# Tiles of a two-layer decoder moved to multiples of 512 bytes in the on-chip memory

## The chip, the cores and the metric

The kernel runs on one core of one Trainium2 chip. Its time is the device time of one execution in microseconds (us). A core has TensorE (PE: matrix products; PEld is its load of the stationary operand), VectorE (DVE), ScalarE (ACT), GpSimd (POOL) and SyncE (SP, which here issues most DMAs). They work side by side, each in the order of its own queue, and share an on-chip memory of 128 partitions. A tile has 128 rows, one to a partition, and takes the same bytes in each; its place is its first byte within the partition.

## The reference

x has 512 tokens of 2,048 channels in float32. Two layers follow each other; each norms x, projects it with one wide matrix, works on the columns by branches, gates the branches with SiLU, projects them back and adds the result to x.

```python
for layer in range(DEPTH):
    h = rmsnorm(x, norm_gains[layer])
    if layer % 2 == 0:
        x = x + even_layer(h, *even_params)
    else:
        x = x + odd_layer(h, *odd_params)
return rmsnorm(x, final_norm_gain)
```

The even layer has a gated linear recurrence (RG-LRU, width 1,024, with a short convolution and two gates) and attention over a window of 128 keys with sinks (16 query heads). The odd layer has multi-head latent attention (MLA: low-rank queries and keys/values, rotary part, 8 heads) and differential attention (two softmaxes of which the second is subtracted, 8 heads). Its projections are all products of 512 tokens with 2,048 (or 768, or 512) channels.

## The kernel before

Activations stand transposed: 128 channels on the partitions, 512 tokens along the row. One output tile of a projection is a `Job`: 16 steps over the 2,048 input channels, at each step the product of a 128x128 block of weights (stationary, loaded into the array) with a 128x512 activation tile (streamed), added up in one bank of the output memory. For the accuracy of float32 from float32r products, each operand is kept as a rounded high part and the rest (low part), and a step is three products (`mm3`): high·high, high weight·low activation, low weight·high activation.

Weights come as pieces of 128x1024 (`Piece`). A piece is loaded into a tile `wr`; ScalarE copies it rounded into `wh`, VectorE subtracts into `wl`. These three have three buffers each in the pool `wts`. Pieces that are used twice at the end ("kept") and those of the MLA values are split into ordinary work tiles instead (`sh`, `sl`). All activations, their high and low parts (`sh`/`sl`, `yh`/`yl`, `ch`/`cl`, `xh`/`xl`, `kh`/`kl`), scores and probabilities are work tiles of 2,048 bytes: 76 buffers of the pool `work`. The gates of the recurrence have their own pool `gatew`: `xp` (the convolution's input with three columns of zeros ahead), `gw` (gate weights) and `gh`, `gl` (their parts). The opening differs from the rest: the first two output tiles (`o`) are computed with both operands in work tiles, while x and the first weights (`fr`) arrive.

The order of instructions on PE, ACT and DVE is written by the program itself: a small planner with fixed costs runs the tasks of the attention branches between the steps of the jobs. Where a tile lies is no part of the plan.

The pools lie one behind the other in the order in which they are made: `const`, `wts`, `gatew`, `work`, `tiny`. A tile takes its size, rounded up to 32 bytes. So the sizes in `const` and `gatew` decide where the tiles behind them begin. Before the change `const` holds, among others, `cc` (constants: identity, ones, masks, cosines), `onesr`, `g0`, `idle` (zeros for the nine warm-up products at the start) and, made later, `junk` (an output nobody reads).

In a row of the profile `mm<-sh,wh` means: output tile mm, streamed operand sh, stationary operand wh. `mm`, `o`, `sc` and `pt` are the output banks. All instructions pass through one line of a helper (L61), so groups are told apart by tiles.

Of the kernel before, what the change touches and what calls it, by code (L numbers as in the profile page):

```python
# [9 lines left out]
F32 = mybir.dt.float32  # L10
# [5 lines left out]
P = 128  # L16
S = 512
# [6 lines left out]
NSLOT = 76  # L24
WARM = 9
DEBUG = False


C_G0, C_G1, C_GF = 0, 16, 32
# [162 lines left out]
def trunk_kernel(ctx: ExitStack, tc, xT, w0, w0o, wg, w1, wuq, wuk, wuv, w1o, small, cst, outT):  # L192
# [11 lines left out]
    gp = ctx.enter_context(tc.tile_pool(name="gatew", bufs=2))  # L204
# [9 lines left out]
    def nm(s):  # L214
        count[0] += 1
        return f"{s}_{count[0]}"
# [7 lines left out]
    def const(n, name, dt=F32):  # L224
        return cp.tile([P, n], dt, name=nm(name))[:, :]
# [172 lines left out]
    def big_job(wt, m, X, done, pre=None, norm=None, kept=(False, False), tag="mm"):  # L398
        return Job(big_parts(wt, m, kept), X, done, pre, norm, tag)
# [73 lines left out]
    pool.memset(nhalf, -0.5)  # L473
    onesr = const(P, "onesr", F32R)
    g0 = const(KT, "g0")

    def col(c):
        return sm[:, c : c + 1]


    idle = const(P, "idle")
    dve.memset(idle, 0.0)
    warm = bank("sc")
    for _ in range(WARM):
# [56 lines left out]
    def parameters():  # L541
# [37 lines left out]
        dve.tensor_tensor(hp, hp, sr, ALU.mult)  # L579
        dve.scalar_tensor_tensor(sp4, hp, 2.0, relu, ALU.mult, ALU.add)  # L580
        dve.tensor_scalar(sp4, sp4, 4.0, None, ALU.mult)

    junk = const(P, "junk")

    def evac(acc, norm, name):
        z = wk(name)
        dve.tensor_tensor(z, acc, norm.r, ALU.mult)
        return z
# [62 lines left out]
    def lru(t, xp, gw):  # L651
        xc = wk("xc")
        cw = [col(C_CW + 8 * j + t) for j in range(4)]
        yield after(xp, sp4)
        dve.tensor_scalar(xc, xp[:, 0:S], cw[0], col(C_CB + t), ALU.mult, ALU.add)
        for j in range(1, 4):
            dve.scalar_tensor_tensor(xc, xp[:, j : j + S], cw[j], xc, ALU.mult, ALU.add)
        gh = gp.tile([P, 2 * P], F32R, name=nm("gh"), tag="gh", bufs=1)[:, :]
        gl = gp.tile([P, 2 * P], F32R, name=nm("gl"), tag="gl", bufs=1)[:, :]
        high(gh, gw)  # L660
        yield after(gh, xc)
        low(gl, gw, gh)
        xh, xl = wk("xh", F32R), wk("xl", F32R)
        high(xh, xc)
        yield after(xh)
        low(xl, xc, xh)
        yield after(xl)
        gi, th = wk("gi"), wk("th")
        for j, (dst, b) in enumerate(((gi, C_GXB), (th, C_GAB))):
            a = []  # L670
            yield from take("sc", a)
            mm3(a[0], gh[:, j * P : (j + 1) * P], gl[:, j * P : (j + 1) * P], (xh, xl), True, True)
            yield after(a[0])
            act.activation(dst, a[0], AF.Sigmoid, bias=col(b + t))
            give("sc", a[0])
        act.activation(th, th, AF.Tanh, scale=sp4[:, t : t + 1])
        yield after(gi)
        dve.scalar_tensor_tensor(gi, gi, 2.0, xc, ALU.mult, ALU.mult)
        yield after(th)
        rec = wk("rec")  # L680
        dve.tensor_scalar(rec, th, 1.0, None, ALU.add)
        dve.reciprocal(rec, rec)
        sq = wk("sqt")
        act.activation(sq, th, AF.Sqrt)
        yield after(sq, rec)
        dve.tensor_tensor(sq, sq, rec, ALU.mult)
        dve.tensor_scalar(rec, rec, 2.0, -1.0, ALU.mult, ALU.add)
        dve.tensor_tensor(gi, gi, sq, ALU.mult)
        h = wk("h")
        dve.tensor_tensor_scan(h, rec, gi, 0.0, ALU.mult, ALU.add)  # L690
        hs[t] = h
# [111 lines left out]
    def gates0(t, za, zb):  # L803
        while t not in hs or t not in os_:
            yield plan.now + 0.5
        yield after(za, zb)
        act.activation(za, za, AF.Silu)
        act.activation(zb, zb, AF.Silu)
        yield after(za, hs[t])
        dve.tensor_tensor(za, hs[t], za, ALU.mult)  # L810
        yield after(zb, os_[t])
        dve.tensor_tensor(zb, os_[t], zb, ALU.mult)
        Y0[2 * t] = za
        Y0[2 * t + 1] = zb
        hs[t] = os_[t] = 0

    def layer0_jobs(t):
        def x_done(acc):
            xp = gp.tile([P, S + 4], F32, name=nm("xp"), tag="xp", bufs=1)[:, :]
            dve.memset(xp[:, 0:3], 0.0)  # L820
            dve.tensor_tensor(xp[:, 3 : 3 + S], acc, n0.r, ALU.mult)
            gw = gp.tile([P, 2 * P], F32, name=nm("gw"), tag="gw")[:, :]
            pool.dma_start(gw, wg[t])
            plan.spawn(lru(t, xp, gw))

        def q_done(acc):
            plan.spawn(swa(t, evac(acc, n0, "qz")))

        zs = []

        def g_done(acc):
            zs.append(evac(acc, n0, "gz"))
            if len(zs) == 2:
                plan.spawn(gates0(t, *zs))

        big_job(w0, 2 + 4 * t, X0, x_done, None, n0)
        big_job(w0, 4 + 4 * t, X0, q_done, None, n0)
        yield
        big_job(w0, 3 + 4 * t, X0, g_done, None, n0, tag="mm" if t else "pt")
        big_job(w0, 5 + 4 * t, X0, g_done, None, n0)  # L840
        yield
# [510 lines left out]
    for i, j in enumerate(jobs):  # L1352
# [3 lines left out]
        elif j is not skip:  # L1356
            j.run()
        if DEBUG:
            print("job", i, "%.1f" % plan.now)
# [128 lines left out]
```

## Time and profile before

| | |
|---|---|
| median of 3 runs | 1594.34 us (1594.31 to 1594.49) |
| the profiled execution | 1594.0 us |
| its span, first to last instruction | 1592.2 us |
| mean granted TensorE clock | 0.997 |
| PE busy | 1576.4 us (99%), 7,450 products |
| PEld busy | 1296.6 us (81%) |
| DVE busy | 867.1 us (54%) |
| ACT busy | 705.2 us (44%) |
| DMA | 156.11 MB, mean 98 GB/s |

A product's listed duration runs from its start to the end of its writing; the next one starts before that end. How fast PE gets through a row of products is therefore read from their starts, or from a window: its length over the number of products that start in it. In a window's row the columns are PE, PEld, DVE, ACT and POOL, each with its busy time and the number of instructions that ran in it, then the granted clock, the DMA engines' busy share and GB/s.

### The profile page before, as it was taken

What the parts mean: (1) busy time and instruction counts of PE and PEld (TensorE: products, weight loads), DVE (VectorE), ACT (ScalarE), POOL (GpSimd) and SP (SyncE); (2) the same over time, 40 slices, a digit from 0 to 9 for tenths busy, and PEclk for the clock granted to TensorE, in tenths of its full rate; (3) what the DMA queues carried; (4) which work ended last, traced back from release to release, by engine and by line L of the source; (5) the groups of instructions that cost most, each with busy time, mean ns of one, the idle gap of its engine ahead of it and who ended that gap; (6) DMA issues with size and microseconds to landing.
All of it is one profiled execution on the core that took longest, in us unless ns stands there. A gap on an engine that the chain in (4) does not pass through costs nothing.

```text
span 1592.2 us, 19224 instructions
## 1 busy us (share of the span) xinstructions
PE 1576.4 (99%) x7450; PEld 1296.6 (81%) x7450; DVE 867.1 (54%) x1603; ACT 705.2 (44%) x1219; POOL 48.2 (3%) x76
## 2 busy tenths in 40 slices
PE   9999999999999999999999999999999999999996
PEld 7888888888888888888888888888888888888886
DVE  7877676677853334455445555542344365843344
ACT  7466455556643323444444454432323356632222
POOL 0000000000001100000000000000000000010000
PEclk9999999999999999999999999999999999999998
DMA  8222232222334443222222222222322221342323
GB/s 282 87 78 91 80 96 83 83 80 80 102 117 147 136 152 105 89 82 83 87 80 79 80 82 89 81 80 93 95 91 86 77 75 55 113 139 93 97 89 106
DMA packets 48922, 156.11 MB, mean 98 GB/s; under 512 B 5552, under 2 KB 9792, under 8 KB 48704
## 3 DMA queue, kind: packets, MB, share of 16 engines
q1 hardware_dynamic: 44576, 141.25, 27.8%
q0 software_dynamic: 4256, 13.64, 2.6%
q8 instruction: 58, 0.95, 0.2%
q14 instruction: 32, 0.26, 0.1%
HBM read 146.49 MB, written 8.39 MB: 97 GB/s over the span
## 4 chain that ended last, share of the span: by engine, by line
PE 97%; issue 1%; DVE 1%; DMA 0%; SPq 0%; POOLq 0%; ACT 0%; POOL 0%; DVEq 0%
PE mm L61 85%; PE o L61 5%; PE sc L61 5%; PE pt L61 3%; DMA xin<-in_xT 0%; DVE st L61 0%; SPq L61 0%; DVE sl L61 0%; POOLq L1483 0%; ACT sh L61 0%; POOL rcf L61 0%; DVE mg L61 0%; DVE yl L61 0%; DVE dg L61 0%; DVEq L1483 0%
## 5 line engine op out<-in xcount | busy, mean ns | idle before, releaser
L61 DVE TENSOR_TENSOR wl<-wr,wh 128x1024 fp32r<-128x1024 f32 (+1 forms) x244 | 290.9, 1192 | 436.3 <-ACT wh L61 436.1
L61 PE MATMUL mm<-sh,wh 128*128 128x512 f32 x1312 | 528.2, 403 | 0.0
L61 PE MATMUL mm<-sl,wh 128*128 128x512 f32 x1312 | 518.4, 395 | 0.0
L61 PE MATMUL mm<-sh,wl 128*128 128x512 f32 x1312 | 518.4, 395 | 0.0
L61 ACT ACTIVATE wh<-wr 128x1024 fp32r<-128x1024 f32 (+1 forms) x244 | 252.2, 1034 | 425.1 <-PE mm L61 342.2
L61 PEld LDWEIGHTS mm<-sh,wl 128*128 128x128 f32 x1312 | 246.2, 188 | 59.3
L61 PEld LDWEIGHTS mm<-sh,wh 128*128 128x128 f32 x1312 | 246.8, 188 | 50.7
L61 PEld LDWEIGHTS mm<-sl,wh 128*128 128x128 f32 x1312 | 246.8, 188 | 50.2
L61 PE MATMUL mm<-yh,wh 128*128 128x512 f32 x448 | 177.7, 397 | 0.0
L61 PE MATMUL mm<-yh,wl 128*128 128x512 f32 x448 | 177.1, 395 | 0.0
L61 PE MATMUL mm<-yl,wh 128*128 128x512 f32 x448 | 177.1, 395 | 0.0
L61 DVE CUSTOM_DVE_ANT_0 p<-sc,cc 128x128 f32<-128x128 f32 (+3 forms) x96 | 47.0, 490 | 98.8 <-PE sc L61 98.6
L61 PEld LDWEIGHTS mm<-yh,wl 128*128 128x128 f32 x448 | 84.1, 188 | 20.4
L61 PEld LDWEIGHTS mm<-yh,wh 128*128 128x128 f32 x448 | 84.1, 188 | 20.1
L61 PEld LDWEIGHTS mm<-yl,wh 128*128 128x128 f32 x448 | 84.1, 188 | 20.0
L61 ACT ACTIVATE p<-p,negm 128x128 f32<-128x128 f32 (+3 forms) x96 | 53.8, 560 | 68.9 <-DVE negm L61 67.4
L61 ACT ACT_TABLE_LOAD x50 | 64.2, 1283 | 1.5 <-PEq L1479 0.7
L61 ACT ACTIVATE aT<-pt 128x128 f32<-128x128 f32 (+3 forms) x64 | 27.6, 435 | 62.0 <-PE pt L61 61.8
L61 ACT ACTIVATE sq<-xr 128x512 f32<-128x512 f32 (+1 forms) x33 | 19.3, 586 | 55.1 <-DVE xr L61 55.1
L61 PE MATMUL mm<-ch,wh 128*128 128x512 f32 x104 | 42.0, 404 | 0.0
L61 DVE TENSOR_TENSOR ss<-ss,sq 128x512 f32<-128x512 f32 (+1 forms) x54 | 36.0, 667 | 10.2 <-ACT sq L61 9.4
L61 PE MATMUL mm<-cl,wh 128*128 128x512 f32 x104 | 41.1, 395 | 0.0
(253 smaller groups left out, 1820.4 us busy)
## 6 DMA issues: line engine op xcount, KB each, us to landing
wr<-in_w SPq DMA_DIRECT2D x166, 512.0 KB, 3.5
wr<-in_w0o SPq DMA_DIRECT2D x32, 512.0 KB, 3.6
wr<-in_w1o SPq DMA_DIRECT2D x32, 512.0 KB, 3.5
wr<-in_wuq SPq DMA_DIRECT2D x12, 384.0 KB, 3.1
xin<-in_xT SPq DMA_DIRECT2D x16, 256.0 KB, 5.4
xr<-in_xT POOLq DMA_DIRECT2D x16, 256.0 KB, 3.7
x1d<-xr POOLq DMA_DIRECT2D x16, 256.0 KB, 3.5
xr<-x1d POOLq DMA_DIRECT2D x16, 256.0 KB, 3.0
```

Source lines behind the costliest of these rows:

```text
L61: return f(*args, **kw)
```

## The change

Three things are done to places; the instructions of every engine and their order stay as they were, but for the name of one tile. `idle` and `junk` become one tile, made where `idle` was. A tile of 96 columns (384 bytes) that nothing uses, `gap`, is put into `const`. `xp` gets 128 columns more than its 512 instead of 4.

```diff
+XPAD = 128
...
     g0 = const(KT, "g0")
+    const(96, "gap")
...
-    idle = const(P, "idle")
+    idle = junk = const(P, "junk")
     dve.memset(idle, 0.0)
...
-    junk = const(P, "junk")
-
...
-            xp = gp.tile([P, S + 4], F32, name=nm("xp"), tag="xp", bufs=1)[:, :]
+            xp = gp.tile([P, S + XPAD], F32, name=nm("xp"), tag="xp", bufs=1)[:, :]
```

Where the first buffers begin, worked out from the sizes of all tiles (bytes within a partition, and what is left over a multiple of 512):

| tiles | before | rest | after | rest |
|---|---|---|---|---|
| cc | 18112 | 192 | 18112 | 192 |
| onesr | 26336 | 224 | 26336 | 224 |
| wr, wh, wl (each buffer 4,096) | 28288 | 128 | 28160 | 0 |
| xp | 65152 | 128 | 65024 | 0 |
| gw, gh, gl (each 1,024) | 67232 | 160 | 67584 | 0 |
| work tiles (each 2,048) | 71328 | 160 | 71680 | 0 |

Sizes of wts, gw and work buffers are multiples of 512, so what holds for the first buffer holds for all, and for each 128-column block (512 bytes) within one.

## The prediction

> **What bounds the kernel now.** I read the page's busy shares and the chain that ended last first, to see which engine sets the end; then the groups of instructions by shape, to see what that engine does; then the timeline and windows of TensorE, to measure the step from one product's start to the next. The last is needed because products are pipelined: their listed durations overlap.
>
> ```profile
> PE 1576.4 (99%) x7450; PEld 1296.6 (81%) x7450; DVE 867.1 (54%) x1603; ACT 705.2 (44%) x1219; POOL 48.2 (3%) x76
> PEclk9999999999999999999999999999999999999998
> PE 97%; issue 1%; DVE 1%; DMA 0%; SPq 0%; POOLq 0%; ACT 0%; POOL 0%; DVEq 0%
> PE mm L61 85%; PE o L61 5%; PE sc L61 5%; PE pt L61 3%; DMA xin<-in_xT 0%; DVE st L61 0%; SPq L61 0%; DVE sl L61 0%; POOLq L1483 0%; ACT sh L61 0%; POOL rcf L61 0%; DVE mg L61 0%; DVE yl L61 0%; DVE dg L61 0%; DVEq L1483 0%
> L61 PE MATMUL mm<-sl,wh 128*128 128x512 f32 x1312 | 518.4, 395 | 0.0
> L61 PE MATMUL mm<-yl,wh 128*128 128x512 f32 x448 | 177.1, 395 | 0.0
> L61 PE MATMUL mm<-cl,wh 128*128 128x512 f32 x104 | 41.1, 395 | 0.0
> ```
>
> TensorE carries 97% of the chain, at a granted clock of nine tenths or more in all slices but the last, and 85% of the chain is one kind of work: 512-wide products into "mm" with a streamed operand from the work pool (sh, sl, yh, yl, ch, cl) and stationary weights from a weight piece (wh, wl). Each of the three groups shown has two sisters of the same count, so there are 3 x (1312 + 448 + 104) = 5,592, and 48 more into "pt": 5,640. A change acts through the step of these 5,640 products or hardly at all.
>
> That step has two values in this trace:
>
> ```profile
> 15.31 0.39 PE L61 MATMUL o<-sh,sl 128*128 128x512 f32 x1
> ...
> 28.91 0.39 PE L61 MATMUL o<-sh,sl 128*128 128x512 f32 x1
> ```
>
> ```profile
> 15.30:28.90 13.60, 13.60 (x61) 11.27 (x60) 12.77 (x20) 11.62 (x20) 0.00 (x0) 1.00 0.93 350
> 440.00:620.00 180.00, 180.00 (x773) 144.81 (x772) 75.32 (x89) 57.78 (x72) 15.03 (x28) 1.00 0.42 135
> 1259.18:1267.57 8.39, 8.39 (x38) 6.95 (x37) 3.21 (x6) 3.40 (x6) 0.00 (x0) 1.00 0.17 50
> ```
>
> A window counts the product already running at its start, so x61 is 60 starts. In the opening, where streamed and stationary operand both lie in the work pool (160 bytes past a multiple of 512), 13.60 us / 60 = 226.7 ns. In the output projection of layer 0, with the stationary operand in a weight piece (128 past), 180.00 / 772 = 233.2 ns. In the MLA value products, both operands in the work pool again, 8.39 / 37 = 226.8 ns. All are 512-wide, at clock 1.00. The fast opening is the busiest stretch of all (DVE 12.77 and ACT 11.62 of 13.60 us, DMA share 0.93), the slow one is quieter, so other engines and transfers are not what costs the 6.5 ns. Nor is the output bank: the value products fill one bank for twelve products, as the slow ones do for 48.
>
> The cleanest piece of evidence is a few products of the recurrence's gates (gh and gl lie at 160) that stand inside the stream of weight pieces:
>
> ```profile
> 67.07 0.40 PE L61 MATMUL mm<-sh,wl 128*128 128x512 f32 x1
> 67.31 0.39 PE L61 MATMUL sc<-xh,gh 128*128 128x512 f32 x1
> 67.53 0.39 PE L61 MATMUL sc<-xl,gh 128*128 128x512 f32 x1
> 67.76 0.40 PE L61 MATMUL sc<-xh,gl 128*128 128x512 f32 x1
> 67.99 0.40 PE L61 MATMUL mm<-sh,wh 128*128 128x512 f32 x1
> ```
>
> ```profile
> 67.54 0.19 PEld L61 LDWEIGHTS sc<-xh,gl 128*128 128x128 f32 x1
> 67.76 0.19 PEld L61 LDWEIGHTS mm<-sh,wh 128*128 128x128 f32 x1
> L61 PE MATMUL sc<-xh,gh x16: 388/390/398, 67.3 to 390.1; 128*128 128x512 f32 x16
> L61 PE MATMUL sc<-xh,gl x16: 390/396/397, 67.8 to 390.6; 128*128 128x512 f32 x16
> ```
>
> The load of the next stationary operand (PEld) starts with the running product: gl is loaded from 67.54 under xl·gh, which began at 67.53; the next wh from 67.76 under xh·gl. A product under which a tile at 160 is loaded takes 390 ns, like the fast stretches; the third, under which a wh at 128 is loaded, 396 ns. (The timeline's starts round to 10 ns; these medians show the 6 ns better.) So the slow step goes with the place of the operand being loaded, against that of the one being streamed.
>
> **The change part by part.** Instructions, order, waits and transfers stay; only places in the on-chip memory move.
>
> Weight pieces go from 128 to 0 past a multiple of 512, work tiles and gate weights from 160 to 0. Streamed and loaded operand of every big product then have the same place within 512 bytes, as in the fast stretches. If that sameness is what counts, each of the 5,640 steps goes from 233.2 to 226.7 ns: 6.5 x 5,640 = 36.7 us less. That is on the path, since PE is 97% of it. Not all will come, because the fast step does not always set in at once after another shape:
>
> ```profile
> 1329.70 0.39 PE L61 MATMUL mm<-sl,ch 128*128 128x512 f32 x1
> ...
> 1330.63 0.39 PE L61 MATMUL mm<-sh,cl 128*128 128x512 f32 x1
> ```
>
> Between these starts lie four steps, with both operands at 160, just after transposes: 0.93 / 4 = 232 ns. In the timeline of PE the 512-wide products stand in 428 runs; 1,568 products are among the first six of a run, 938 among the first three. With no gain but 1.2 ns on the first six, 4,072 x 6.5 + 1,568 x 1.2 = 28.4 us; the gates, where the fast step sets in at once, speak for the full 36.7. Middle: 32 us.
>
> The 256-wide products of the tail and of the scores go the other way, or stay:
>
> ```profile
> 1542.46 0.28 PE L61 MATMUL mm<-yh,sh 128*128 128x256 f32 x1
> ...
> 1547.98 0.28 PE L61 MATMUL mm<-yl,sh 128*128 128x256 f32 x1
> 1542.45:1547.99 5.54, 5.54 (x49) 5.54 (x48) 3.67 (x5) 2.63 (x4) 0.00 (x0) 1.00 0.01 3
> 1553.78 5.61 PE o L61 x48
> ```
>
> With both operands in the work pool (two of the 49 were already running, so 47 starts and 46 steps) it is 5.52 / 46 = 120.0 ns; with wh at 128 (48 in the chain's last row) 5.61 / 48 = 116.9. Only 96 products are of the second kind: 96 x 3.1 = +0.3 us.
>
> VectorE and ScalarE: their operands move as well. The split of a kept piece reads at 128 and writes at 160, a sum of squares has all at 160, and they take the same:
>
> ```profile
> L61 DVE TENSOR_TENSOR sl<-wr,sh 128x512 fp32r<-128x512 f32 x20 | 12.8, 686 | 3.1 <-ACT sh L61 3.1
> L61 DVE TENSOR_TENSOR ss<-ss,sq 128x512 f32<-128x512 f32 x50 | 34.4, 687 | 9.3 <-ACT sq L61 8.4
> L61 DVE TENSOR_TENSOR wl<-wr,wh 128x1024 fp32r<-128x1024 f32 x224 | 273.9, 1223 | 409.4 <-ACT wh L61 409.2
> ```
>
> I cost them at nothing. Their cover is TensorE itself: the split of the pieces waits 409 us in all for the copy ahead of it, which in turn waits for work of PE, so a PE faster by 2% leaves DVE at 867 / 1560 = 56%. The one tile that now serves for warm-up and scratch, the gap and the wider xp add no instruction: nothing.
>
> Sum, against the profiled execution's own 1594.0 us (span 1592.2 and 1.8 around it; the median of the runs is 1594.34): 1594.3 - 32 + 0.3 = 1562 us, or 1558 to 1566 between the two bounds.
>
> The bounds of what no row shows, a product whose streamed operand starts at a multiple of 64 or more: every streamed float32r operand here starts at 160. From 256 to 512 columns the fast step grows by 226.7 - 120.0 = 106.7 ns, so columns alone are 213.4 of the 226.7 ns and 13.3 ns stand on top in both. The lower bound is that these vanish, the upper that nothing changes or that the 3.1 ns of the 256-wide products are added. I take 226.7, the value that same-place operands have.
>
> [...]
>
> **The rivals.** First, more than the fast step. The 13.3 ns on top may come from the streamed tile's odd start itself: if the memory is read in pieces of 64 bytes (sixteen columns), 2,048 bytes from 160 touch one piece more than from 0, and sixteen columns cost 213.4 x 16 / 512 = 6.7 ns, half of the 13.3. If one such piece goes, about 6,700 products of 256 columns and more (5,640, and some 1,050 from the work and gate pools) save 6.7 ns beside the 32 us: 45 us more, 1517. If all 13.3 go, 89 us, 1473. For it: 13.3, and the 6.5 of the slow step, are nearly whole multiples of 6.7. Against: the constant is as well explained by the load, and no row has an aligned stream.
>
> [...]
>
> Second, no change. The load may be slow at even multiples of 64 bytes (128 now, 0 then) and fast at odd halves (160), whatever the stream does; then the 5,640 steps stay at 233.2 and it is 1594. For it: the trace varies only the loaded operand, never the streamed one. Against: a worse time for the rounder place would be odd, unless two streams meet.
>
> Third, slower. The 256-wide products lose 3.1 ns where places agree. If agreement costs that in every product, and the fast stretches are fast for the odd start of their load, the big steps go to 236.3: 5,640 x 3.1 = 17.5 us, 1612. It decides once the step is over 233.8 ns (3.2 us / 5,640 = 0.6 ns more). For it the tail's rows, against it the 226.8 of the value products, whose places agree.
>
> **How the numbers follow.** The fast step taking over, 1558 to 1566: 0.47. More than that, 1473 to 1550: 0.33 (most of it near 1517, 0.05 below 1487). Part of it, because the fast step seldom sets in after an interruption, 1568 to 1590: 0.05. No change: 0.08. Slower: 0.07. A measurement of this kernel can tell about 0.2%, 3.2 us. Faster 0.85, same 0.08, slower 0.07. The likeliest gives 1562. The range leaves out the two last cases and the lowest of the second: 1487 to 1590.
>
> **What would show it.** Right: windows at the output projections with 226.7 ns a step or less, the listed 395 ns of mm<-sl,wh at 390 or less, VectorE's 686 and 1223 ns as they were, PE still 97% of the chain. The 96 tail products at 120 say that agreement is the rule. [...] I am wrong if PE's step falls and the span does not, because waits of PE on DVE or ACT, which hardly show in the chain now, take its place.

## The result, and the profile after

| | before | after |
|---|---|---|
| median | 1594.41 us (1594.31 to 1595.1, 4 runs) | 1567.35 us (1565.43 to 1567.61, 4 runs) |
| the profiled execution | 1594.0 us | 1567.61 us |
| its span | 1592.2 us | 1565.8 us |

The ratio is 0.9827, 95% interval 0.981 to 0.9844: 27 us less. 1562 had been forecast, with 1558 to 1566 for the likeliest case; the time lies just past that and inside the range.

The page's first line and its chain say that the bound is the same engine:

```profile
PE 1549.5 (99%) x7450; PEld 1297.9 (83%) x7450; DVE 866.4 (55%) x1603; ACT 705.2 (45%) x1219; POOL 48.2 (3%) x76
...
PE 97%; issue 1%; DVE 1%; DMA 0%; SPq 0%; POOLq 0%; ACT 0%; POOL 0%; DVEq 0%
```

PE's busy time fell by 26.9 us, DVE's by 0.7 and ACT's not at all. The groups of products and of VectorE's splits (mean duration after the busy time):

```profile
L62 PE MATMUL mm<-sl,wh 128*128 128x512 f32 x1312 | 512.0, 390 | 0.0
L62 PE MATMUL mm<-yl,wh 128*128 128x512 f32 x448 | 174.5, 389 | 0.0
L62 PE MATMUL mm<-cl,wh 128*128 128x512 f32 x104 | 40.6, 391 | 0.0
L62 DVE TENSOR_TENSOR sl<-wr,sh 128x512 fp32r<-128x512 f32 x20 | 12.8, 686 | 3.1 <-ACT sh L62 3.1
L62 DVE TENSOR_TENSOR wl<-wr,wh 128x1024 fp32r<-128x1024 f32 x224 | 273.6, 1222 | 392.5 <-ACT wh L62 392.3
```

The three kinds of big product that took 395 ns take 389 to 391; the splits take what they took (686 and 1223 ns before). A window inside the output projection of layer 0 and the pieces of the chain that hold the long stretches give the step. The chain before, for comparison:

```profile
437.57 189.00 PE mm L61 x810
...
1059.28 103.58 PE mm L61 x444
```

The window and the chain after:

```profile
440.00:600.00 160.00, 160.00 (x707) 132.30 (x706) 67.08 (x79) 51.13 (x63) 14.49 (x27) 1.00 0.44 142
```

```profile
432.55 183.75 PE mm L62 x810
...
1043.03 100.69 PE mm L62 x444
...
1527.51 5.76 PE o L62 x48
```

160.00 / 706 = 226.6 ns a step, where it was 233.2. The same 810 products that took 189.00 us of the chain take 183.75. The last row is the tail's 48 products of 256 columns: 5.76 / 48 = 120.0 ns, where it was 116.9.

### The profile page after: what moved, and what is told of

Read it like the earlier page. It is cut to its first block, busy times and chain, and to the rows that moved or that the text cites. A ratio compares the mean times of both kernels' runs of the same rounds, so it can differ in the third digit from the quotient of the medians.

```text
span 1565.8 us, 19224 instructions
## 1 busy us (share of the span) xinstructions
PE 1549.5 (99%) x7450; PEld 1297.9 (83%) x7450; DVE 866.4 (55%) x1603; ACT 705.2 (45%) x1219; POOL 48.2 (3%) x76
## 3 DMA queue, kind: packets, MB, share of 16 engines
q1 hardware_dynamic: 44576, 141.25, 28.4%
## 4 chain that ended last, share of the span: by engine, by line
PE 97%; issue 1%; DVE 1%; DMA 0%; SPq 0%; POOLq 0%; ACT 0%; POOL 0%; DVEq 0%
PE mm L62 84%; PE o L62 5%; PE sc L62 5%; PE pt L62 4%; DMA xin<-in_xT 0%; DVE st L62 0%; SPq L62 0%; DVE sl L62 0%; POOLq L1483 0%; ACT sh L62 0%; POOL rcf L62 0%; DVE mg L62 0%; DVE yl L62 0%; DVE dg L62 0%; DVEq L1483 0%
## 5 line engine op out<-in xcount | busy, mean ns | idle before, releaser
L62 PE MATMUL mm<-sh,wh 128*128 128x512 f32 x1312 | 522.5, 398 | 0.0
L62 PE MATMUL mm<-sh,wl 128*128 128x512 f32 x1312 | 512.3, 390 | 0.0
L62 PE MATMUL mm<-sl,wh 128*128 128x512 f32 x1312 | 512.0, 390 | 0.0
```

The source lines that it names most:

```text
L62: return f(*args, **kw)
```

## The experiments

All of them keep the instructions and their order and differ from the change only in places. The comparison kernel in each is the one before the change. "Place" below is the rest over a multiple of 512 bytes. The chain has in each the piece of 810 products without another shape between them, so its length is the measure of the step: 810 x 226.7 = 183.6 us or 810 x 233.3 = 189.0.

**Which of the places counts.** Two runs take away one half of the change each (the wider `xp`, or `gap`), two put the places elsewhere.

gap_only: weight pieces at 0, gates and work tiles at 32.

```diff
-XPAD = 128
+XPAD = 4
```

> The change without the wider xp: weight pieces at 0 past a multiple of 512, work tiles and gates at 32. Theory P (the step depends on whether the loaded and the streamed operand have the same place): they differ by 32, so 233.2 ns a step at the projections, 1593 to 1596 us, and the 96 tail products with wh at 116.9 ns. Theory W (the loaded operand at a multiple of 512 is enough): 226.7 ns, 1565 to 1568 us.

xp_only: everything at 128.

```diff
-    const(96, "gap")
```

> The change without the gap of 96 columns: weight pieces, gates and work tiles all at 128 past a multiple of 512. Theory P: the places agree, 226.7 ns, 1565 to 1568 us, tail products 120.0 ns. Theory M (the multiple of 512 itself counts, or 128 is a bad place for weights): 233.2 ns, 1593 to 1596 us.

all160: everything at 160.

```diff
-    const(96, "gap")
+    const(136, "gap")
```

> Weight pieces, gates and work tiles all at 160 past a multiple of 512, an odd multiple of 32. Theory P: 226.7 ns, 1565 to 1568 us. Theory M (the multiple of 512, or of 64, counts): 1593 to 1596 us.

w32_x0: weight pieces at 32, gates and work tiles at 0.

```diff
-XPAD = 128
+XPAD = 120
...
-    const(96, "gap")
+    const(104, "gap")
```

> Weight pieces at 32 past a multiple of 512, work tiles and gates at 0. Theory P: they differ by 32, 233.2 ns, 1593 to 1596 us. Theory S (the streamed operand at a multiple of 512 is enough): 226.7 ns, 1565 to 1568 us.

| run | weights | work | median us | ratio to before (95%) |
|---|---|---|---|---|
| gap_only | 0 | 32 | 1593.96 | 0.9997 (0.9988 to 1.0007) |
| xp_only | 128 | 128 | 1566.8 | 0.9829 (0.9814 to 0.9844) |
| all160 | 160 | 160 | 1565.99 | 0.9823 (0.9808 to 0.9837) |
| w32_x0 | 32 | 0 | 1594.55 | 1.0 (0.9991 to 1.001) |

The chain's piece of 810 products and, where shown, the tail's 48, in that order of the runs:

```profile
437.68 188.99 PE mm L62 x810
...
1554.04 5.61 PE o L62 x48
```

```profile
430.63 183.78 PE mm L62 x810
...
1526.01 5.76 PE o L62 x48
```

```profile
431.04 183.78 PE mm L62 x810
```

```profile
438.41 189.00 PE mm L62 x810
...
1554.62 5.67 PE o L62 x48
```

Theory P holds four times out of four. Each half of the change alone either gives nothing (gap_only) or all of it (xp_only), according to whether the places agree. Weights at a multiple of 512 are not enough, work tiles at a multiple of 512 are not enough, and with everything at an odd multiple of 32 the whole gain is there. The price in the tail has the other sign: 5.76 us where places agree, less where they don't (5.61 in gap_only, 5.67 in w32_x0).

**Within what unit they must agree.** The weights at 64, 128 and 256, work tiles at 0 (the gap grows by 64, 128 and 256 bytes, xp shrinks by as much):

```diff
-XPAD = 128
+XPAD = 112    # w64_x0; 96 in w128_x0; 64 in w256_x0
...
-    const(96, "gap")
+    const(112, "gap")    # w64_x0; 128 in w128_x0; 160 in w256_x0
```

> Weight pieces at 64 past a multiple of 512, work tiles and gates at 0. If places need to agree within 64 bytes only (Q64): 226.7 ns a step, 1565 to 1568 us. If they need to agree within 128 to 512 bytes (Q512): 233 ns, 1592 to 1596 us.

> Weight pieces at 128 past a multiple of 512, work tiles and gates at 0. If places must agree within a unit of 128 bytes only: 226.7 ns a step, 1565 to 1568 us. If within 256 or 512: 233.3 ns, 1592 to 1596 us.

> Weight pieces at 256 past a multiple of 512, work tiles and gates at 0. If places must agree within a unit of 256 bytes: 226.7 ns a step, 1565 to 1568 us. If within 512: 233.3 ns, 1592 to 1596 us.

w64_x0 took 1595.8 us (ratio 1.0011, 1.0001 to 1.002), w128_x0 1591.63 us (0.9983, 0.9972 to 0.9994), w256_x0 1565.2 us (0.9815, 0.9787 to 0.9844). Their pieces of the chain:

```profile
438.17 188.99 PE mm L62 x810
```

```profile
437.20 188.22 PE mm L62 x810
```

```profile
429.92 183.79 PE mm L62 x810
```

So of the distances tried the unit is 256 bytes: a difference of 256 is as good as none, 128 is nearly as bad as 64. w256_x0 (two runs) is the fastest median of all, but its interval overlaps that of the change; the two can't be told apart, and no run beats the change beyond that.

**How exactly they must agree.** First try: the buffers of wh and wl 64 bytes longer, the parts 4 or 16 bytes in. It rested on a unit of 64 bytes, which w64_x0 refuted: buffers 64 bytes longer lie at 64, 128, ... to each other, so all but one of the six differ from the work tiles for that reason already. The two runs are inconclusive on what was asked.

```diff
+OFF = 1    # off4B; 4 in off16B
...
-            t = wp.tile([P, 1024], dt, name=nm(tag), tag=tag)[:, :]
+            t = (wp.tile([P, 1024], dt, name=nm(tag), tag=tag)[:, :] if tag == "wr" else
+                 wp.tile([P, 1040], dt, name=nm(tag), tag=tag)[:, OFF : OFF + 1024])
...
-    const(96, "gap")
...
```

The last cut, here and in the second try, is the tile `st` near the end, which uses the same buffers and is lengthened with them.

> High and low weight parts start 4 bytes past a multiple of 64 (each buffer is 64 bytes longer), work tiles at 0. If agreement to the element counts: 233 ns or more, 1592 us or more. If 16 or 32 bytes are the unit in which places agree: 226.7 ns, 1565 to 1568 us.

> High and low weight parts start 16 bytes past a multiple of 64, work tiles at 0. If 32 bytes are the unit: 226.7 ns, 1565 to 1568 us. If 16 bytes or less are the unit: another step than 226.7 ns; between 226.7 and 233.3 if the price grows with the distance, 1567 to 1594 us.

off4B took 1592.3 us (0.9987, 0.9976 to 0.9997), off16B 1591.07 us (0.9982, 0.9972 to 0.9992).

Second try: buffers longer by 512 bytes, so that all places stay equal but for the offset; two work slots fewer pay for the room.

```diff
-NSLOT = 76
+NSLOT = 74
...
+OFF = 1    # far_off4B; 4 in far_off16B
...
-            t = wp.tile([P, 1024], dt, name=nm(tag), tag=tag)[:, :]
+            t = (wp.tile([P, 1024], dt, name=nm(tag), tag=tag)[:, :] if tag == "wr" else
+                 wp.tile([P, 1152], dt, name=nm(tag), tag=tag)[:, OFF : OFF + 1024])
...
```

> Buffers of wh and wl 512 bytes longer (paid for with two work slots fewer, order of instructions unchanged), and the weight parts start 4 bytes past a multiple of 512; work tiles at 0. If one element of distance already counts: 232 to 233.3 ns a step, 1590 to 1596 us. If places are compared in units of 16 or 32 bytes: 226.7 ns, 1565 to 1569 us.

> As the run with 4 bytes, with the weight parts 16 bytes past a multiple of 512. If 16 bytes already count: 232 to 233.3 ns a step, 1590 to 1596 us. If places are compared in units of 32 bytes: 226.7 ns, 1565 to 1569 us.

far_off4B took 1590.31 us (0.9974, 0.9962 to 0.9986), far_off16B 1587.68 us (0.9954, 0.9932 to 0.9977). The chain, 4 bytes first; the piece of 638 holds the output projection of layer 1:

```profile
436.91 188.23 PE mm L63 x810
```

```profile
436.81 189.00 PE mm L63 x810
...
1412.98 134.76 PE mm L63 x638
```

The piece of 638 before the change, and after it:

```profile
1415.43 138.35 PE mm L61 x638
```

```profile
1392.68 134.83 PE mm L62 x638
```

One element of distance costs most of the gain: about 4 us of the 27 are left. With 16 bytes the trace gives two answers. The output projection of layer 0 (the piece of 810) is as slow as before the change, and that of layer 1 is as fast as after it, all through its piece: 134.76 us. That is 3.6 of the 6.8 us by which the run is faster than before, and so a little faster than either branch of the expectation allowed for. At this distance, then, the rest over 256 bytes alone does not decide the step; what does is open. The two work slots fewer had no control of their own.

**Is the price paid load by load.** wl_off32 moves only the low weight parts, by 32 bytes put ahead of them (xp shrinks by as much):

```diff
-XPAD = 128
+XPAD = 120
...
+            if tag == "wl" and not slots[tag]:
+                wp.tile([P, 8], F32, name=nm("pad"), tag="pad", bufs=1)
             t = wp.tile([P, 1024], dt, name=nm(tag), tag=tag)[:, :]
```

> As the change, but with the low parts wl alone at 32 past a multiple of 512 (32 unused bytes ahead of them); everything else at 0. One load in three then differs from the stream. If each load prices the product that runs over it (D): a mean step of (2 x 226.7 + 233.3) / 3 = 228.9 ns, 5,640 / 3 x 6.6 = 12 us over the change, 1577 to 1581 us. If one load that differs spoils the steps that follow (T): 232 to 233 ns, 1588 to 1595 us.

It took 1592.91 us (0.9992, 0.9982 to 1.0001). The chain, a window at the output projection of layer 0, the groups of products between 445 and 600 us, and four products of that stretch:

```profile
437.61 188.98 PE mm L62 x810
```

```profile
440.00:600.00 160.00, 160.00 (x687) 128.64 (x686) 67.69 (x81) 52.13 (x65) 13.99 (x26) 1.00 0.41 135
```

```profile
L62 PE MATMUL mm<-yl,wh 128*128 128x512 f32 x222 | 88.8, 400 | 0.0
L62 PE MATMUL mm<-yh,wh 128*128 128x512 f32 x222 | 87.7, 395 | 0.0
L62 PE MATMUL mm<-yh,wl 128*128 128x512 f32 x222 | 86.4, 389 | 0.0
```

```profile
502.77 0.40 PE L62 MATMUL mm<-yl,wh 128*128 128x512 f32 x1
503.01 0.39 PE L62 MATMUL mm<-yh,wl 128*128 128x512 f32 x1
503.24 0.40 PE L62 MATMUL mm<-yh,wh 128*128 128x512 f32 x1
503.47 0.40 PE L62 MATMUL mm<-yl,wh 128*128 128x512 f32 x1
```

The product under which wl is loaded (yl·wh) takes 400 ns, the one after it 389 and the third 395. The starts go the same way: the median step over this projection is 239 ns after the start of yl·wh, 228 after yh·wl and 233 after yh·wh. So the price is not the same at every step: it is doubled under the load that is out of place, nearly nothing at the next step and single at the third. The mean is 160.00 / 686 = 233.2, as if every load were out of place. Of the two expectations the number of T came out, and D's 228.9 did not; T's picture, one bad load that makes all following steps slow, did not come out either. Why the three steps add up to the full price is open.

## Why the prediction was right, and where it was off

**The bound** was read rightly: PE carries 97% of the chain before and after, and no wait took the place of what went. That the time lies inside 1487 to 1590 says little by itself, since the lower part of that range was there for a rival that did not come true; what bears the prediction out is the step. No run shows a step that would lead to the range's lower end of 1487 us or below it; the whole gain came with 226.6 to 226.9 ns.

**The step.** 226.7 ns was taken from the opening and the value products; 226.6 was measured. That the gain comes from agreement, and not from round places, is shown by xp_only and all160 against gap_only and w32_x0. The gates' products, which had no neighbour of another place after the change, went the same way, the third kind from a median of 396 to 389:

```profile
L62 PE MATMUL sc<-xh,gh x16: 388/389/396, 68.6 to 385.7; 128*128 128x512 f32 x16
L62 PE MATMUL sc<-xh,gl x16: 389/389/397, 69.2 to 386.2; 128*128 128x512 f32 x16
```

"Within 512 bytes" was too coarse (the unit is 256), and the gates' rows read as a price paid by the product under the load: wl_off32 shows the price largest there (239 ns), but paid by another product of the three as well, so that it can't be counted load by load.

**The term that was mis-sized** is the one for short runs of products. The prediction took 32 us, the middle between 28.4 (no full gain on the first six of a row) and 36.7. The upper bound rested on the gates, and these do not bear on the term: 15 of their 16 groups stand behind other 512-wide products, not behind another shape. The lower bound was the better reading: added up over the timeline's PE rows, the 5,640 products take 28.6 us less (mean step 235.1 ns before, waits between included, 230.0 after). (In the trace before, the 5,640 stand in 277 rows with 1,539 of them among the first six, which puts that bound at 28.5 us; the prediction's 1,568 fits a count over all 6,040 products of 512 columns.) The fast step needs some five products to set in even when all places agree: over all rows of 512-wide products after the change, the median steps from the second product on are 235, 233, 232, 229.5 and then 227 ns, where before they were 230 to 234 throughout. The first step, 314 ns, is the same in both. After one interruption, all operands at 0:

```profile
674.96 0.49 PE L62 MATMUL pt<-cc,p 128*128 128x128 f32 x3
675.20 0.48 PE L62 MATMUL mm<-sh,wh 128*128 128x512 f32 x1
675.52 0.40 PE L62 MATMUL mm<-sl,wh 128*128 128x512 f32 x1
...
676.45 0.39 PE L62 MATMUL mm<-sh,wl 128*128 128x512 f32 x1
676.68 0.49 PE L62 MATMUL o<-v,aT 128*128 128x128 f32 x3
```

From 675.52 to 676.45 are four steps, 0.93 / 4 = 232 ns; then the next interruption comes. The chain shows the sum of such places: the piece of 810 gained 5.25 of 189.00 us (2.8%), and the stretch from its end (437.57 + 189.00 = 626.57 us before, 432.55 + 183.75 = 616.30 after) to the piece of 444 (from 1059.28 before), which is full of interruptions, went from 432.71 us to 1043.03 - 616.30 = 426.73 us, 5.98 us or 1.4%.

**The tail** went to 120.0 ns as forecast: +0.3 us.

**What no term held:** the opening of the profiled execution came 2.2 us later than before. PE waited for work on a late piece of x, and the granted clock halved for a while:

```profile
8.55 1.35 ACT L62 ACTIVATE sh<-xin,g 128x512 fp32r<-128x512 f32 x2 [2.29 <-DMA xin<-in_xT]
...
9.32 0.51 PE L62 MATMUL o<-sh,sh 128*128 128x512 f32 x1 [1.31 <-ACT sh L62]
...
32.01 0.39 PE L62 MATMUL mm<-sh,wh 128*128 128x512 f32 x1
```

```profile
11.36:14.77 3.41, 3.41 (x10) 2.65 (x8) 2.71 (x5) 3.41 (x7) 0.00 (x0) 0.50 1.06 405
```

The first product of the projections starts at 32.01 where it was 29.82:

```profile
29.82 0.39 PE L61 MATMUL mm<-sh,wh 128*128 128x512 f32 x1
```

The agreement of places does not bring this about: in w256_x0, whose operands agree as well, that product starts at 29.39 and the mean clock is 0.996. The mean clock in the profile of the change, 0.995, is the lowest of the fourteen (0.996 or 0.997 in the others); in the trace before, the clock was 1.00 from 5.53 to 1582.40 us.

```profile
29.39 0.39 PE L62 MATMUL mm<-sh,wh 128*128 128x512 f32 x1
```

So the profiled sum is 28.6 less, 0.3 more in the tail, 2.2 more in the opening: 26.1, against 26.4 us between the two spans. Whether the other executions of the change had a late opening too is not known. Two of them took nearly as long as the profiled one (1567.41 and 1567.29 us), the third 1565.43, about as long as w256_x0.

**The rivals.** More than the fast step: refuted as it was worked out. all160 streams from 160, the change from 0, and both have the same step (183.78 and 183.75 us for 810 products), so the 13.3 ns that the prediction put on top of the columns don't come from an odd start. No long stretch came clearly below 226.6 ns a step. No change: refuted by the time, and the idea behind it (the load's own place) by gap_only and xp_only, in which weights at 0 are slow (1593.96 us) and at 128 fast (1566.8). Slower: its rows in the tail were right, its extension to 512 columns was not (226.6 ns where it had 236.3).

The placements say that load and stream are not independent of each other: medians of 1565 to 1568 us in the four kernels whose places agree or differ by 256 bytes, 1587 to 1596 in the ten others.

**Still open:** by what mechanism the places matter (the runs show that they do, not how); why a row of equal products needs five of them before the fast step; why 256-wide products prefer disagreement; why 16 bytes cost the full price in one output projection and nothing in the other.

## What to carry to other kernels

Where TensorE bounds the kernel with a new stationary block at each product, try to put stationary and streamed tiles at the same rest over 256 bytes, all of them: one tile in three elsewhere lost the gain (1592.91 us in wl_off32, 1567.35 with all in place). This was seen with float32r products of 512 columns; those of 256 columns lost 1 to 3 ns by it (120.0 ns against 116.9 in gap_only and 5.69 us / 48 = 118.5 in w128_x0). The pools' order and the odd sizes ahead of them decide this silently, and one wider tile can set it right. Read the step from starts or windows over a long row of equal products, and compare two places of the same program that differ in one thing: here 6 ns in the gates' products foretold 27 us.

## What the runs showed of the hardware that was not expected

- Places that differ by 256 bytes are as good as equal ones: 1565.2 us against 1565.99 to 1567.35. Distances of 32 to 128 bytes lose nearly all of the gain (1591.63 to 1595.8 us), and 4 bytes still most of it (1590.31).
- At a distance of 16 bytes one output projection ran at the slow step (189.00 us for its 810 products) and the other at the fast one (134.76 us for its piece of 638, where it was 138.35 before and 134.83 after).
- One load in three out of place by 32 bytes brings the mean step to 233.2 ns, as if all were, with steps of 239, 228 and 233 ns in turn.
- 256-wide products are the other way round: 120.0 ns where places agree, 116.9 to 118.1 where they differ by 32 bytes.
- After a wait of 1.31 us in one opening the granted clock was 0.50 from 11.36 to 14.77 us. The mean clock in that profile, 0.995, is the lowest of the fourteen (0.996 or 0.997 in the others); that the wait brought the fall about is not shown.
